# S5's input products on x times the norm's weights; the root and the shift's product applied to their results

## The chip, the cores and the metric

The kernel runs on one core of a Trainium2 chip. The metric is the time of one execution on the device in microseconds. Three runs of the kernel before gave 2488.64, 2485.32 and 2486.29 us, a median of 2486.29.

A core has five engines, each with a queue of its own that runs in the order in which it was written: PE (TensorE, matrix products into PSUM), DVE (VectorE), ACT (ScalarE), POOL (GpSimdE) and SP (SyncE, which here only issues DMA transfers). They wait for one another by semaphores.

## The reference, cut to what matters

x has 512 tokens of 1024 channels. A first network (pool mixer, feed-forward, attention, feed-forward) is followed by a second one, whose first layer is an S5 mixer on a modulated norm of x. Only the lines around the border of the two matter here:

```python
x = x + rms_norm(f, ffn_post_g[layer])            # end of the first network, f from ffn1
...
mod = cond @ ada_w[i] + ada_b[i]                  # cond = silu(c), six parts of 1024 each
sh1, sc1, g1, sh2, sc2, g2 = jnp.split(mod[:, None, :], N_MOD, axis=-1)
h = _modulate(_rmsnorm(x, norm_mix_g[i]), sh1, sc1)   # x * root * g * (1 + sc1) + sh1
...
u = (h @ w_in).astype(f32)                        # S5's input product, w_in is 1024 x 1024
```

With root the reciprocal root of a token's mean square, h @ w_in equals root * ((x * g * (1 + sc1)) @ w_in) + sh1 @ w_in. The root is one number a token, sh1 @ w_in one number a channel.

## The kernel before

x is held transposed: eight tiles xT of 128 channels by 512 tokens. A product in float32 accuracy is made of three matrix products (mm3, L217 to L220): weights and data are each split into a rounded part and the rest (wh and wl; hi and lo), and wh by hi, wh by lo and wl by hi are added in PSUM. Weights come in chunks of 128 x 1024 (wchunk, L178): SP loads ws, ACT makes wh (L203), DVE wl (L204). There are three ws buffers and four each of wh and wl. S5's w_in is split with its columns permuted (perm, L198 to L200), so its reads go in steps of 16 elements.

Between two layers stands a seam (L785). It works by halves of 256 tokens, called half 0 and half 1 here. The layer before finishes its products (for ffn1: tl.run, evacuated by DVE at L979 and squared by ACT at L294, DVE adding up at L295). Then post_add (L426) takes the root of the feed-forward's result, scales it (u, L434) and adds it to xT (L437). A root is made by Norm.rs (L297): PE sums the squares over the channels (L303), ACT takes the root (L305), DVE inverts it and spreads it on a diagonal (L306, L309), and PE spreads it over the partitions (L312); the PSUM tile for it, pn, exists once.

For S5, the seam's second part is a PreNorm (L362): after post_add it needs the squares of the new x, a second root, and then for each of eight tiles u = x * gs * root (DVE, L388), h = u + shift (ACT, L391) and the rest of h (DVE, L392). Only then can the first products of S5 (head, L1406) begin. Elsewhere, before ffn0, attention and ffn1, the seam has a PreScale (L404): it splits x times the norm's weights (L418, L419) in step with post_add, tile by tile, and the root is made later and kept in rsx (L424), to be applied to the products.

S5's head makes four of the eight output tiles of w_in for half 0, then for half 1; the body (L1431) makes the other four for all 512 tokens. u_out (L1331) copies each from PSUM to usc (L1336), writes it to DRAM (d_u) and reads it back in another layout (U), from which states (L1352, products L1360) starts.

The vector mod is made during ffn1 by a background generator: ada_units (L503) calls vecmat (L466), which multiplies rows of ada_w by numbers of cond on DVE. For each of 12 column blocks it takes 8 loads of 256 KB into two buffers (as, L483) and 8 steps (L486, L488) into one accumulator aa; then three rounded copies ab (L496) with two subtractions (L498); then 12 small matrix products into pn (L472) that add over the partitions, and DVE's sum (L475). The blocks not made during ffn1's body are drained before the seam. The order of each engine's queue is fixed when the program is built, by a scheduler that simulates it.

Of the kernel before, what the change touches and what calls it, by code (L numbers as in the profile page):

```python
# [11 lines left out]
F32 = mybir.dt.float32  # L12
# [3 lines left out]
AF = mybir.ActivationFunctionType  # L16
ALU = mybir.AluOpType
# [4 lines left out]
P = 128  # L22
# [3 lines left out]
KD = D // P  # L26
# [36 lines left out]
def net_kernel(ctx: ExitStack, tc: tile.TileContext, I: dict, out: bass.AP, parts=ALL):  # L63
    nc = tc.nc
    V, A, G, T = nc.vector, nc.scalar, nc.gpsimd, nc.tensor

    cst = ctx.enter_context(tc.tile_pool(name="cst", bufs=1))
# [10 lines left out]
    def nm(s):  # L78
        uid[0] += 1
        return f"{s}_{uid[0]}"  # L80
# [4 lines left out]
    def tt(s="t", dt=F32):  # L85
        return tp.tile([P, S], dt, tag="t", name=nm(s))

    def ht(s="h", dt=F32R):
        return hp.tile([P, S], dt, tag="h", name=nm(s))
# [11 lines left out]
    V.memset(ones, 1.0)  # L101
    one16 = cst.tile([P, 1], BF16, name="one16")
    V.memset(one16, 1.0)
    eps1 = cst.tile([P, 1], F32, name="eps1")
    V.memset(eps1, 1e-6)
    eps2 = cst.tile([P, 1], F32, name="eps2")
    V.memset(eps2, 1e-5)
    mod = cst.tile([P, 96], F32, name="mod")
    cond = cst.tile([P, KD], F32, name="cond")
    cond_set = []  # L110
    recent = {}

    nrow = sum(n for _, n in VECS)
    vec = cst.tile([P, nrow], F32, name="vec")
    voff = {}
# [36 lines left out]
    def vc(name, i):  # L152
        o = voff[name] + i
        return vec[:, o:o + 1]

    def md(i, m, k):
        c = i * 48 + m * 8 + k
        return mod[:, c:c + 1]
# [81 lines left out]
    class Held:  # L240
# [3 lines left out]
        def __init__(self, runs):  # L244
            self.runs, self.ch, self.ap = runs, {}, {}
# [109 lines left out]
    def behind(instructions):  # L355

        with ExitStack() as stack:
            for ins in instructions:
                stack.enter_context(tc.issue_after(ins))
            yield  # L360

    class PreNorm:  # L362

        late = False

        def __init__(self, norm, eps, modulate):
            self.norm, self.eps, self.modulate = norm, eps, modulate
            self.h = None
            i, m, gname = modulate
            self.gs = cst.tile([P, KD], F32, tag="gs", bufs=2, name=nm("gs"))  # L370
            c = i * 48 + (m + 1) * 8
            go = voff[gname] + 8 * i
            V.scalar_tensor_tensor(self.gs, mod[:, c:c + 8], 1.0, vec[:, go:go + 8], ALU.add, ALU.mult)

        def parts(self, span):
            return ()
# [27 lines left out]
    class PreScale(PreNorm):  # L404

        late = True

        def __init__(self, norm, eps, gain=None):
            self.norm, self.eps, self.gain = norm, eps, gain
            self.h = [(ht(), ht()) for _ in range(KD)]  # L410
            self.rs = None

        def parts(self, span):

            ts = slice(*span)
            g = [1.0 if self.gain is None else vc(self.gain[0], self.gain[1] + k) for k in range(KD)]
            hi, lo = ([h[i][:, ts] for h in self.h] for i in range(2))
            return (lambda k: A.activation(hi[k], xT[k][:, ts], AF.Copy, scale=g[k]),  # L418
                    lambda k: V.scalar_tensor_tensor(lo[k], xT[k][:, ts], g[k], f(hi[k]), ALU.mult, ALU.subtract))  # L419
# [43 lines left out]

    def vecmat(pool, W, ncb, col, done):  # L466

        def total(parts, cb):
            ps = psn.tile([P, 512], F32, tag="n", name=nm("pn"))
            for j in range(3):  # L470
                for q in range(4):
                    T.matmul(ps[:, 4 * q + j:4 * q + j + 1], parts[j][:, q * P:(q + 1) * P], one16,  # L472
                             start=True, stop=True)
            sums = cst.tile([P, 4], F32, tag="asum", bufs=2, name=nm("sums"))
            V.tensor_reduce(sums, ps[:, :16].rearrange("p (q j) -> p q j", q=4)[:, :, :3], AX.X, ALU.add)  # L475
            done(cb, sums)

        due = None
        for cb in range(ncb):
            acc = None  # L480
            for k in range(KD):
                st = pool.tile([P, 512], F32, tag="as", bufs=2, name=nm("as"))
                nc.sync.dma_start(st, W[k * P:(k + 1) * P, cb * 512:(cb + 1) * 512])  # L483
                if k == 0:
                    acc = pool.tile([P, 512], F32, tag="aa", bufs=1, name=nm("aa"))
                    V.tensor_scalar(acc, st, col(k), None, ALU.mult)  # L486
                else:
                    V.scalar_tensor_tensor(acc, st, col(k), acc, ALU.mult, ALU.add)  # L488
                if k % 2:
                    yield  # L490
                if k == 1 and due is not None:
                    total(*due)
            t2 = tt("ab").bitcast(BF16)
            parts = [t2[:, :512], t2[:, 512:], pool.tile([P, 512], BF16, tag="ab", bufs=1, name=nm("ab"))]
            for j in range(3):
                A.activation(parts[j], acc, AF.Copy)  # L496
                if j < 2:
                    V.tensor_tensor(acc, acc, parts[j], ALU.subtract)  # L498
            due = parts, cb
        yield  # L500
        total(*due)

    def ada_units(pool, i):  # L503

        if not cond_set:
            cond_set.append(True)
            c0 = voff["c_2"]
            with behind([recent["split"]]):
                A.activation(cond, vec[:, c0:c0 + KD], AF.Silu)
            yield  # L510

        def done(cb, sums):
            c = i * 48 + cb * 4
            bo = voff["ada_b_2"] + c
            V.tensor_tensor(mod[:, c:c + 4], sums, vec[:, bo:bo + 4], ALU.add)

        yield from vecmat(pool, I["ada_w_2"][i], 12, lambda k: cond[:, k:k + 1], done)

    def s5_tables(pool, dr):

# [789 lines left out]
    def s5_layer(dr, pool, pa):  # L1310
        S_ = {"gh": [None] * KD, "gl": [None] * KD}
# [19 lines left out]
        def u_out(n, ps, span=FULL):  # L1331
            if span[0] == 0:
                U[n] = tt("usc")
            usc = U[n]
            cs = slice(span[0] // 8, span[1] // 8)
            a = A.activation(usc.rearrange("p (s c) -> p s c", s=8)[:, :, cs], ps.rearrange("p (c s) -> p s c", s=8),  # L1336
                             AF.Copy)
            S_["lastu"] = [a.ins]
            if span[1] < S:
                return  # L1340
            nc.scalar.dma_start(dr["u"][n].rearrange("s (h g c) -> (h g) s c", h=16, g=8),
                                usc.rearrange("p (s c) -> p s c", s=8))
            U[n] = at("U")
            nc.sync.dma_start(U[n], dr["u"][n].rearrange("s (h j) -> (s h) j", h=16))
# [130 lines left out]
        def tail_(hf, nxt):  # L1475
# [23 lines left out]
            for q in range(2):  # L1499
                glu(6 + q, pp[0][:, 256 * q:256 * q + 256], pp[1][:, 256 * q:256 * q + 256], HALVES[hf])  # L1500

        return Layer(lambda nxt: PreNorm(nxt, eps2, (0, 0, "norm_mix_g_2")), load, head, body_, tail_,
                     lambda span, nxt, pre: None)


# [394 lines left out]
    names = [p for p in parts if p != "final"]  # L1900
# [29 lines left out]
        bgps[0] = psmm  # L1930

    rope_c = {}
    s5_on = "s5" in names
    ada_on = [any(p in names for p in q) for q in (("s5", "mlp0"), ("ssd", "mlp1"))]
    ada_due = [i for i in range(2) if ada_on[i]]
    tables_due, toeplitz_due = s5_on, s5_on
# [70 lines left out]
    nxt = None if names[-1] in ("mlp0", "mlp1", "s5", "ssd") else Norm()  # L2007
# [32 lines left out]
```

## Time and profile before

| | |
|---|---|
| median of three runs | 2486.29 us |
| the profiled execution's own time | 2485.38 us |
| its span, first to last instruction | 2483.7 us |
| what lies around the span | 1.7 us |
| PE busy | 2340.7 us, 94% of the span |
| DVE busy | 1713.8 us, 69% |
| ACT busy | 1142.1 us, 46% |
| mean granted TensorE clock | 0.972 |

PE is the engine that sets the time: it is busy nearly throughout, and the places where it stands still are few. One is the seam between ffn1 and S5, from about 1102 to 1185 us of the span. In rows of stretches, each engine's busy time is followed by its instructions in brackets, and PEclk is the granted clock as a share of 2.4 GHz. In rows of the chain the two numbers are the start and the length of a piece in us. Where a row has square brackets, they hold the idle time ahead of the instruction and what ended it.

### The profile page before, as it was taken

The numbers are of one execution on the slowest core, as the hardware profiler recorded it, in microseconds if no ns is written. First come the engines' busy times: TensorE is split into PE (matmuls) and PEld (weight loads), VectorE is DVE, ScalarE is ACT, GpSimd is POOL, SyncE is SP. The second block draws the span as 40 slices with busy tenths as digits, with TensorE's granted clock in tenths as the row PEclk, the third lists the DMA queues.
The fourth block names the chain that finished last, engine by engine and source line by source line (L and its number), as shares of the span: only waits on it lengthen the run. The fifth ranks groups of instructions, "written<-read, shape, count | busy, mean of one in ns | idle before, by whom it ended". The sixth has DMA issues, their size and how long they took to land.

```text
span 2483.7 us, 33557 instructions
## 1 busy us (share of the span) xinstructions
PE 2340.7 (94%) x12397; PEld 1972.1 (79%) x12397; DVE 1713.8 (69%) x3069; ACT 1142.1 (46%) x2038; POOL 337.9 (14%) x345
## 2 busy tenths in 40 slices
PE   7999999788979999986899999999999999999998
PEld 7877777776778888875878887889878888888888
DVE  6896989678658778786655666666777788633333
ACT  6543535467665444344543433334555554422332
POOL 1001223201200000000110210110143331200110
PEclk9999999889989999997999999999999999999999
DMA  4224443311274555552942455543433332232222
GB/s 122 88 88 140 131 142 103 125 52 51 75 206 134 180 178 165 179 173 68 306 153 77 143 166 191 188 134 92 125 105 99 107 104 80 93 102 94 95 88 72
DMA packets 297780, 311.29 MB, mean 125 GB/s; under 512 B 53569, under 2 KB 251025, under 8 KB 296593
## 3 DMA queue, kind: packets, MB, share of 16 engines
q1 hardware_dynamic: 270033, 278.22, 36.0%
q10 hardware_dynamic: 23680, 17.31, 2.3%
q0 software_dynamic: 3904, 13.63, 1.7%
q8 instruction: 97, 1.59, 0.3%
q14 instruction: 66, 0.54, 0.1%
HBM read 284.92 MB, written 24.18 MB: 124 GB/s over the span
## 4 chain that ended last, share of the span: by engine, by line
PE 74%; DVE 12%; DMA 6%; ACT 4%; issue 3%; SPq 0%; POOL 0%; DVEq 0%; ACTq 0%; POOLq 0%
PE mm L219 22%; PE mm L218 22%; PE mm L220 22%; DMA as<-in_ada_w 3%; DVE wl L204 3%; ACT wh L203 1%; DVE aa L488 1%; PE mm L1642 1%; PE mm L1643 1%; PE mm L1644 1%; PE pb L1712 1%; PE pb L754 1%; DMA tz<-d_k 1%; ACT th L775 1%; DMA d_u<-usc 1%
## 5 line engine op out<-in xcount | busy, mean ns | idle before, releaser
L218 PE MATMUL mm<-h,wh 128*128 128x512 f32 (+1 forms) x1792 | 665.6, 374 | 22.9 <-ACT h L418 7.2
L219 PE MATMUL mm<-h,wh 128*128 128x512 f32 (+1 forms) x1792 | 666.1, 372 | 6.2 <-DVE h L392 3.3
L220 PE MATMUL mm<-h,wl 128*128 128x512 f32 (+1 forms) x1792 | 664.8, 372 | 1.7 <-DVE wl L204 1.7
L203 ACT ACTIVATE wh<-ws 128x1024 fp32r<-128x1024 f32 (+1 forms) x367 | 388.0, 1060 | 563.3 <-PE mm L219 479.6
L204 DVE TENSOR_TENSOR wl<-ws,wh 128x1024 fp32r<-128x1024 f32 (+1 forms) x367 | 466.0, 1272 | 240.7 <-ACT wh L203 234.3
L218 PEld LDWEIGHTS mm<-h,wh 128*128 128x128 f32 x1792 | 346.8, 194 | 81.0 <-issue 8.5
L219 PEld LDWEIGHTS mm<-h,wh 128*128 128x128 f32 x1792 | 347.1, 194 | 63.3 <-DVE h L392 5.4
L220 PEld LDWEIGHTS mm<-h,wl 128*128 128x128 f32 x1792 | 347.3, 194 | 56.3 <-DVE wl L204 2.5
L218 PE MATMUL mm<-hi,wh 128*128 128x512 f32 (+1 forms) x1056 | 369.5, 354 | 9.0 <-ACT wh L203 7.6
L219 PE MATMUL mm<-lo,wh 128*128 128x512 f32 (+1 forms) x1056 | 372.0, 353 | 1.7 <-DVE lo L319 1.7
L220 PE MATMUL mm<-hi,wl 128*128 128x512 f32 (+1 forms) x1056 | 370.8, 353 | 0.8 <-DVE wl L204 0.8
L218 PEld LDWEIGHTS mm<-hi,wh 128*128 128x128 f32 x1056 | 200.6, 190 | 37.3 <-ACT wh L203 8.7
L219 PEld LDWEIGHTS mm<-lo,wh 128*128 128x128 f32 x1056 | 201.4, 191 | 28.5 <-DVE lo L319 2.7
L220 PEld LDWEIGHTS mm<-hi,wl 128*128 128x128 f32 x1056 | 201.2, 191 | 26.8 <-DVE wl L204 1.0
L488 DVE SCALAR_TENSOR_TENSOR aa<-as,cond,aa 128x512 f32<-128x512 f32 x168 | 132.0, 786 | 113.8 <-DMA as<-in_ada_w 112.3
L1266 POOL TENSOR_TENSOR r<-r 128x512 f32<-128x512 f32 x64 | 88.1, 1379 | 671.1 <-ACT r L1262 488.0
L760 POOL TENSOR_TENSOR dd<-ident,s5dg 16x64 f32<-16x64 f32 x16 | 69.4, 4337 | 343.1 <-DVE kt L762 336.1
L319 DVE TENSOR_TENSOR lo<-r,hi 128x512 fp32r<-128x512 f32 x64 | 48.1, 756 | 76.5 <-ACT hi L317 76.4
L1287 DVE SCALAR_TENSOR_TENSOR x<-mm,mod,x 128x512 f32<-128x512 f32 (+1 forms) x76 | 48.9, 662 | 60.6 <-PE mm L220 60.4
L496 ACT ACTIVATE ab<-aa 128x512 bf16<-128x512 f32 x72 | 44.9, 624 | 97.0 <-DVE aa L488 61.7
L317 ACT ACTIVATE hi<-r 128x512 fp32r<-128x512 f32 x64 | 40.4, 631 | 72.3 <-POOL r L1266 72.3
L295 DVE TENSOR_TENSOR acc<-acc,sq 128x256 f32<-128x256 f32 (+1 forms) x148 | 62.0, 432 | 16.4 <-ACT sq L294 11.6
(484 smaller groups left out, 3651.2 us busy)
## 6 DMA issues: line engine op xcount, KB each, us to landing
ws<-in_mlp_w SPq DMA_DIRECT2D x124, 512.0 KB, 4.0
as<-in_ada_w SPq DMA_DIRECT2D x192, 256.0 KB, 3.1
ws<-in_ffn_w_in SPq DMA_DIRECT2D x88, 512.0 KB, 3.8
ws<-in_m_w_in SPq DMA_DIRECT2D x41, 512.0 KB, 3.7
ws<-in_ffn_w_out SPq DMA_DIRECT2D x40, 512.0 KB, 3.5
ws<-in_w_o SPq DMA_DIRECT2D x16, 512.0 KB, 3.4
ct<-d_tab SPq DMA_DIRECT2D x8, 1024.0 KB, 9.5
ws<-in_s_w_glu SPq DMA_DIRECT2D x16, 512.0 KB, 5.8
```

What stands on the lines that cost most here:

```text
L203: A.activation(h_, s_, AF.Copy)
L204: V.tensor_tensor(l_, s_, f(h_), ALU.subtract)
L218: T.matmul(ps, wh, xh, start=first, stop=False)
L219: T.matmul(ps, wh, xl, start=False, stop=False)
L220: return T.matmul(ps, wl, xh, start=False, stop=last).ins
L295: V.tensor_tensor(dst, dst, sq[:, a:b], ALU.add)
L319: return hi_, V.tensor_tensor(lo[:, ts], src, f(hi[:, ts]), ALU.subtract)
L488: V.scalar_tensor_tensor(acc, st, col(k), acc, ALU.mult, ALU.add)
L496: A.activation(parts[j], acc, AF.Copy)
L760: G.tensor_tensor(dd, ident[:16, :16].unsqueeze(1).broadcast_to([16, 4, 16]), dg[:, g4].unsqueeze(2).broadcast_to([16, 4, 16]), ALU.mult)
L1266: G.tensor_tensor(r, r, r, ALU.mult)
L1287: V.scalar_tensor_tensor(xT[n][:, ts], ps, md(i, 5, n), xT[n][:, ts], ALU.mult, ALU.add)
```

## The change

S5 takes a PreScale in place of its PreNorm: hi and lo are now parts of x times gs, with gs = g * (1 + sc1), made in step with post_add. The root of x is made later and stored in rsx. A further call of vecmat, behind the twelve blocks of the first mod, multiplies w_in by the shift (two column blocks, 16 loads of 256 KB), with its three copies and two subtractions in the permuted order of the columns; the result is s5c. u_out now multiplies a product by rsx on DVE (new L1356) and adds s5c on ACT (new L1357). The eps constants move into one tile.

```diff
+    def modulated(i, m, gname):
+        gs = cst.tile([P, KD], F32, tag="gs", bufs=2, name=nm("gs"))
+        c = i * 48 + (m + 1) * 8
+        go = voff[gname] + 8 * i
+        V.scalar_tensor_tensor(gs, mod[:, c:c + 8], 1.0, vec[:, go:go + 8], ALU.add, ALU.mult)
+        return gs
...
-        def __init__(self, norm, eps, gain=None):
-            self.norm, self.eps, self.gain = norm, eps, gain
+        def __init__(self, norm, eps, gain=None, modulate=None):
+            self.norm, self.eps = norm, eps
+            if modulate is not None:
+                gs = modulated(*modulate)
+                self.gain = lambda k: gs[:, k:k + 1]
+            else:
+                self.gain = lambda k: 1.0 if gain is None else vc(gain[0], gain[1] + k)
...
+            pv, av = parts, acc
+            if perm:
+                pv = [p_.rearrange("p (a h g) -> p a h g", h=16, g=8) for p_ in parts]
+                av = acc.rearrange("p (a g h) -> p a h g", g=8, h=16)
             for j in range(3):
-                A.activation(parts[j], acc, AF.Copy)
+                A.activation(pv[j], av, AF.Copy)
                 if j < 2:
-                    V.tensor_tensor(acc, acc, parts[j], ALU.subtract)
+                    V.tensor_tensor(av, av, pv[j], ALU.subtract)
...
         yield from vecmat(pool, I["ada_w_2"][i], 12, lambda k: cond[:, k:k + 1], done)
+        if i == 0 and s5_on:
+            yield from vecmat(pool, I["s5_w_in_2"][0], 2, lambda k: md(0, 0, k),
+                              lambda cb, sums: V.tensor_copy(s5c[:, 4 * cb:4 * cb + 4], sums), perm=True)
...
-            a = A.activation(usc.rearrange("p (s c) -> p s c", s=8)[:, :, cs], ps.rearrange("p (c s) -> p s c", s=8),
-                             AF.Copy)
+            t = tt("us")[:, :span[1] - span[0]]
+            V.tensor_tensor(t, ps, S_["pre"].rs[:, slice(*span)], ALU.mult)
+            a = A.activation(usc.rearrange("p (s c) -> p s c", s=8)[:, :, cs], t.rearrange("p (c s) -> p s c", s=8),
+                             AF.Identity, bias=s5c[:, n:n + 1])
...
-        return Layer(lambda nxt: PreNorm(nxt, eps2, (0, 0, "norm_mix_g_2")), load, head, body_, tail_,
+        return Layer(lambda nxt: PreScale(nxt, eps2, modulate=(0, 0, "norm_mix_g_2")), load, head, body_, tail_,
```

Up to the last loads of ada_w in the seam, every queue stands as before. From there on the order differs at three places of weight. PE, end of ffn1's last products, before (mm<-hi,wh are ffn1's products, pn the sums and spreads of a root, mm<-h,wh the first products of S5):

```order
L219 MATMUL mm_10606<-lo_10067,wh_10029 128x256
L220 MATMUL mm_10606<-hi_10066,wl_10030 128x256
L312 MATMUL pn_10356<-dg_10362,ones 128x128 x2
L303 MATMUL pn_10430<-ones,acc_10391 128x128 x2
L312 MATMUL pn_10430<-dg_10436,ones 128x128 x2
L218 MATMUL mm_10793<-h_10414,wh_10752 128x256
```

The root of half 0 is there spread right behind ffn1's last product; its sums (L303) stand 35 products earlier, among them. The same place of the change (line numbers are up by 2 here, and L484 is vecmat's product, before L472):

```order
L484 LDWEIGHTS ab_10215
L484 MATMUL pn_10221<-one_86,ab_10215 128x1
L305 MATMUL pn_10468<-ones,acc_10309 128x128 x2
L314 MATMUL pn_10468<-dg_10474,ones 128x128 x2
L220 MATMUL mm_10860<-h_10247,wh_10819 128x256
L220 MATMUL mm_10917<-h_10247,wh_10831 128x256
L221 MATMUL mm_10860<-h_10248,wh_10819 128x256
L222 MATMUL mm_10860<-h_10247,wl_10820 128x256
```

The sums for half 0's root, now L305, have moved behind all of ffn1's products and behind the 24 small products of the two blocks of s5c; the second root (of x) has gone from between them and S5's products.

ACT at the same place in the change (ab_10167 is the last copy of vecmat's first block of s5c, ab_10214 and ab_10215 the three of its second; acc and sq are the squares of ffn1's half 0, the second acc the first square of half 1; L307 is the root):

```order
L512 ACTIVATE ab_10167<-aa_10143 128x512
L512 ACTIVATE ab_10214<-aa_10175 128x512
L293 ACTIVATE acc_10309<-f_8045 128x256
L296 ACTIVATE sq_10312<-f_8056 128x256
...
L296 ACTIVATE sq_10461<-f_8330 128x256
L296 ACTIVATE sq_10465<-f_8346 128x256
L293 ACTIVATE acc_10309<-f_8045 128x256
L512 ACTIVATE ab_10214<-aa_10175 128x512
L512 ACTIVATE ab_10215<-aa_10175 128x512
```

In the order before, these squares stood behind the first copy of the last block of ada_w; now they stand behind the first copy of the last block of s5c, and so of all that is added up for it.

PE between S5's head and its body, in the change (mm<-... 128x256 is the last of the head for half 1, 128x512 the first of the body):

```order
L220 MATMUL mm_11035<-h_10261,wh_10837 128x256
L221 MATMUL mm_11035<-h_10262,wh_10837 128x256
L222 MATMUL mm_11035<-h_10261,wl_10838 128x256
L314 MATMUL pn_10806<-dg_10812,ones 128x128 x2
L220 MATMUL mm_11112<-h_10247,wh_11115 128x512
L221 MATMUL mm_11112<-h_10248,wh_11115 128x512
```

Before, the body's first product followed the head's last one directly. Now the spread of half 1's root of x, L314, stands between them. DVE in the change, where that root is inverted and put on its diagonal (wl are splits of w_in for the body):

```order
L206 TENSOR_TENSOR wl_11116<-ws_11114,wh_11115 128x1024
L206 TENSOR_TENSOR wl_11146<-ws_11144,wh_11145 128x1024
L206 TENSOR_TENSOR wl_11231<-ws_11229,wh_11230 128x1024
L308 RECIPROCAL sr_10809<-sr_10809 128x2
L311 TENSOR_SCALAR dg_10812<-ident,sr_10809 128x128 x2
L1356 TENSOR_TENSOR us_10910<-mm_10860,rsx_10793 128x256
L206 TENSOR_TENSOR wl_11261<-ws_11259,wh_11260 128x1024
```

Before, the splits of w_in for the body stood there alone; now the inversion and the diagonal stand behind three of them.

## Rows read from the trace of the kernel before

**Rows 1.** Stretches: length, busy PE, PEld, DVE, ACT, POOL, PEclk, DMA share, GB/s.
```profile
1102.00:1114.80 12.80, 12.62 (x109) 12.13 (x107) 10.18 (x18) 8.14 (x8) 2.15 (x5) 1.00 0.69 234
1114.80:1131.10 16.30, 2.39 (x8) 1.85 (x8) 12.48 (x31) 4.81 (x12) 0.50 (x1) 0.60 0.57 201
1131.10:1145.60 14.50, 14.47 (x104) 14.16 (x104) 8.71 (x24) 5.52 (x15) 0.00 (x0) 0.87 0.00 0
1145.60:1159.50 13.90, 2.41 (x10) 1.86 (x9) 10.43 (x29) 4.08 (x11) 0.00 (x0) 0.61 0.00 1
1159.50:1173.90 14.40, 14.40 (x96) 14.26 (x97) 7.90 (x16) 8.57 (x15) 2.50 (x7) 0.78 0.10 36
1173.90:1184.80 10.90, 10.90 (x50) 9.02 (x49) 6.62 (x4) 6.12 (x7) 0.00 (x0) 1.00 1.01 281
1199.00:1232.00 33.00, 26.44 (x214) 25.63 (x212) 22.02 (x30) 17.09 (x27) 7.56 (x15) 0.95 0.88 298
```
**Rows 2.** The chain that ended last, 1060 to 1270 us: start, length, what.
```profile
1093.39 2.69 DMA as<-in_ada_w
1096.17 0.75 DVE aa L488
...
1097.62 0.76 DVE aa L488
...
1103.95 2.01 DVE wl L204
...
1115.52 1.88 DVE wl L204
1117.39 0.78 DVE u L434 x2
...
1126.67 1.21 PE pn L303 x4
...
1130.06 0.49 DVE u L388
...
1131.13 0.79 PE mm L218 x2
...
1145.66 0.87 DVE u L434 x2
...
1199.09 13.74 DMA d_u<-usc
```
**Rows 3.** ACT, instructions in time: a permuted and a plain split of weights.
```profile
1113.52 1.96 ACT L203 ACTIVATE wh<-ws 128x1024 fp32r<-128x1024 f32 x1 [3.02 <-PE mm L219]
...
1186.26 1.06 ACT L203 ACTIVATE wh<-ws 128x1024 fp32r<-128x1024 f32 x1 [2.75 <-PE pv L1360]
```
**Rows 4.** Groups by form: count, busy us, mean ns, idle before.
```profile
L496 ACT ACTIVATE ab<-aa 128x512 bf16<-128x512 f32 x72 | 44.9, 624 | 97.0 <-DVE aa L488 61.7 <-DVE aa L498 35.3
L498 DVE TENSOR_TENSOR aa<-aa,ab 128x512 f32<-128x512 f32 x48 | 36.8, 766 | 15.2 <-ACT ab L496 14.8
L294 ACT ACTIVATE sq<-f 128x256 f32<-128x256 f32 x56 | 19.1, 407 | 0.2
```
**Rows 5.** The chain in the seam from attention to ffn1, a PreScale.
```profile
738.34 0.87 DVE u L434 x2
...
741.45 0.58 PE mm L219
...
755.36 1.23 DVE wl L204
...
757.90 0.50 PE mm L218
```
**Rows 6.** Stretches of PE after its stop at 1145.6: length, busy, PEclk, DMA.
```profile
1146.00:1155.00 9.00, 0.00 (x0) 0.65 0.00 0
...
1162.00:1165.00 3.00, 3.00 (x16) 0.50 0.00 0
1165.00:1168.00 3.00, 3.00 (x24) 0.88 0.34 113
```

More of the change, by code (lines that the diff above doesn't have):

```diff
@@ L103, in net_kernel @@
     V.memset(one16, 1.0)
-    eps1 = cst.tile([P, 1], F32, name="eps1")
+    eps = cst.tile([P, 2], F32, name="eps")
+    eps1, eps2 = eps[:, 0:1], eps[:, 1:2]
     V.memset(eps1, 1e-6)
-    eps2 = cst.tile([P, 1], F32, name="eps2")
     V.memset(eps2, 1e-5)
@@ L109, in net_kernel @@
     cond = cst.tile([P, KD], F32, name="cond")
+    s5c = cst.tile([P, KD], F32, name="s5c")
+    s5_on = "s5" in parts
     cond_set = []
@@ L368, in __init__ @@
             self.h = None
[L369 to L373, printed above, removed]
+            self.gs = modulated(*modulate)
         def parts(self, span):
@@ L415, in parts @@
             ts = slice(*span)
-            g = [1.0 if self.gain is None else vc(self.gain[0], self.gain[1] + k) for k in range(KD)]
+            g = [self.gain(k) for k in range(KD)]
             hi, lo = ([h[i][:, ts] for h in self.h] for i in range(2))
@@ L462, in exp_exact, with vecmat @@
         V.scalar_tensor_tensor(x, q, 1.0, b.bitcast(F32), ALU.add, ALU.mult)
-    def vecmat(pool, W, ncb, col, done):
+    def vecmat(pool, W, ncb, col, done, perm=False):
         def total(parts, cb):
@@ L1932, in net_kernel @@
     rope_c = {}
-    s5_on = "s5" in names
     ada_on = [any(p in names for p in q) for q in (("s5", "mlp0"), ("ssd", "mlp1"))]
```

## The prediction

> **What bounds the kernel now.** I read the table of busy times first. PE works in 94% of the span, so a change pays or costs where PE stands still. Then I cut the border between ffn1 and S5 into stretches [rows 1]. PE is filled to 1114.8 by ffn1's last products, stops for 16.3 us with 2.39 busy, works through the head for half 0 (14.5 us), stops for 13.9 us with 2.41 busy, works through the head for half 1 (14.4), and goes into the body without a stop. These two stops are all that the change can shorten here. The chain of waits names what lies in them [rows 2]: u of post_add at 1117.39 (half 0) and at 1145.66 (half 1), after each the eight tiles of x, the sums of x (1126.67), the first tile of the modulated norm (1130.06), and S5's first product (1131.13). From the first u to the body (1173.9) it is 56.5 us.
>
> The same chain, further up, shows the pace of vecmat: two loads of 256 KB, then two products on DVE, then the next two loads into the same two buffers. From the start of a load (1093.39) to the end of its product (1096.17 + 0.75) it is 3.53 us [rows 2], and the next load into that buffer cannot start earlier: with a little for its issue, I count 3.55 us a pair when nothing else is in its way.
>
> **What the change removes.** Between u of post_add and the first product there is no root and no modulated norm any more. A seam of this form is in the trace already, from attention to ffn1 [rows 5]: from u to the first product it is 3.1 us (738.34 to 741.45), where S5 now needs 13.7 (1117.39 to 1131.13). Half 1's root is no longer made beside the head of half 0: the head's stretch counts 104 products against 96 in that of half 1 [rows 1], and eight of them at about 0.1 us, 0.8 us, leave it (13.7 remain). They come back behind the head as a wait. From sums to a scaled u it is 3.4 us in the chain with four sums and eight squares to add (1126.67 to 1130.06); the two sums of half 1 are half of that, and I take 2.5. From u of half 1 to the body the other seam shows 19.6 us (738.34 to 757.90), head and the wait for half 1's root included.
>
> That last wait is new for S5: the spread of half 1's root stands between head and body, and the DVE work for it stands behind three splits of w_in. Those are permuted here. A permuted split takes 1.96 us on ACT and 1.88 to 2.01 on DVE, a plain one 1.06 and 1.23 [rows 2, 3, 5]. One round of ACT and DVE is ahead of the root in the other seam's chain; with its excess of 0.9 and 0.7, and 1.0 for the splits queued ahead of it, I add 2.6. Bounds are 0, if the splits are done while the head still runs, and 4.8, if all three are in the way. The other seam's own wait there included, PE then stops about 3.6 us ahead of the body.
>
> Sum from u of half 0 to the body: 3.1 + 13.7 + 2.5 + 19.6 + 2.6 = 41.5 us, 15.0 less than 56.5.
>
> **What it adds ahead of that.** The order shows the price. All that post_add of half 0 waits for, the squares of ffn1's result on ACT and the sums on PE, now stands behind the vector product for s5c: behind the first copy of its second block on ACT, behind all 24 small products on PE. ffn1's products end by 1114.8 at the latest [rows 1], and from there PE has nothing else. So I follow the vector product in time.
>
> - The last product of ada_w ends at 1098.4 (1097.62 + 0.76). The two first loads of s5c can follow as buffers come free, but DVE has the first split of w_in ahead of their products: first products at about 1104.6.
> - First block, four pairs. Here SP has between the pairs loads of ws that wait for the splits, and DVE has four splits of 1.9 us between the products. A pair costs 1.9 + 1.5 for the products + 0.7 for adding f and squares + about 1 of waiting at the head of SP's queue, about 5 us; without any of that 3.55. Three pairs behind the first end at about 1120.4.
> - Three copies and two subtractions follow one another. The plain ones take 0.624 and about 0.7 us [rows 4]. Permuted like the splits they become 0.624 x 1.96/1.06 = 1.15 and 0.7 x 1.88/1.23 = 1.1, together about 5.3. The end of the first block's copies is at 1125.7.
> - Second block: its first pair is loaded in the meantime, three more at 3.55 end at about 1137.9 (nothing else stands between them in SP or DVE).
> - Behind its first copy come the squares of half 0, about five of 0.407 ahead of the rest [rows 4], then two copies, two subtractions, 12 products and their sum: 5.3 + 1.9 + 0.3. The sums of half 0's root start at 1145.4 or so, and 3.4 us later u at 1148.8.
>
> Against 1117.39 that is 31.4 us later. Bounds: all pairs at 3.55 from the end of ada_w give 1098.4 + 8 x 3.55 + 5.3 + 0.3 for copies and sums and 3.4 for the root, with the squares hidden, = 1135.8, some 1136, 18.8 later; all eight at 5 us put u at 1155, 38 later. I take the middle case, since the first four pairs have the four splits among them and the last four have not.
>
> [...]
>
> **Terms of the later part.** The granted clock: behind the 13.9 us stop PE ran at 0.50, which is 1.2 GHz, and at 0.88 as a mean between 1165 and 1168 [rows 6]; over the whole head the mean was 0.78 [rows 1], and 0.22 of 14.4 us is 3.2 us lost. Of the stop itself nine us had a mean of 0.65 [rows 6], so it fell early in it. The new stop ahead of the body is about 3.6 us long, and the trace shows none of that length ahead of long products: its cost is 0 if the clock holds, 3.2 if it falls. I take 2, nearer the second.
>
> [...]
>
> The evacuation of each tile is now a product on DVE and then ACT, before its transfer to DRAM: about one DVE instruction of 256 columns later (some 0.4 us, as a u) for the last tile; I take 0.5, at most 2, and at least 0. For the tiles before it, these products lie beside PE's work, where DVE is busy 6.62 of 10.9 us in the body and 7.9 of 14.4 in the head [rows 1]; without that cover each costs the same 0.4. Behind that comes the stretch in which S5 itself waits: from 1199 to 1232 PE is busy 26.4 of 33 us at a DMA share of 0.88 [rows 1], and the write of d_u takes 13.74 us [rows 2]. 4 MB of w_in for s5c and the tables (ct) that stand behind them in SP now share the border, where the shares were 0.57 and then 0.00 for the two stops and the head [rows 1]. Loads that ran in that stretch may be done before it, when PE arrives later: up to the 6.6 us that PE stands there could be given back, nothing at the least. I take 1.5 back, near the low end, since d_u's write keeps its length.
>
> **Sum.** 31.4 - 15.0 + 2 + 0.5 - 1.5 = 17.4, about +17 us. The profiled execution took 2485.38 us (2483.7 of span and 1.7 around it), so it becomes 2502.4; the median of the runs is 0.9 above it, so 2503. The bounds of the vector product alone make it +5 and +24; those of the four smaller terms (0 to 4.8, 0 to 3.2, 0 to 2, and 0 to 6.6 off) can move it by another 4 or 5 either way. The case's own range is thus +1 to +29, 2487 to 2515.
>
> **The rivals.**
> 1. *The vector product is hidden (other side).* If the loads run while ffn1's products still fill PE, u of half 0 stays near 1117.4, the 15.0 us are kept, and with +2 and +0.5 the sum is -13, 2473. For it: two buffers are free from 1098, and the transfers stood at 0.69 and 0.57 of their capacity until 1131 [rows 1]. Against it: 16 loads, in pairs of 3.55, need 28.4 us and only 16.4 are left to 1114.8. For the full gain a pair would have to take 0.8 us; the sum changes its sign at 2.5 us a pair, or at 3.0 with plain copies.
> 2. *Only the loads count.* DVE and SP never hold a pair up: 18.8 - 15.0 + 2 + 0.5 - 1.5 = about +5, 2491. For it: DVE was busy only 12.48 of 16.3 us in the first stop [rows 1]. Against it: in the order the splits stand between its products.
> 3. *The loads are slower.* Loads of ws, rot and ct at the same time stretch a pair to 5 us throughout, the clock falls and nothing is given back: 38 - 15.0 + 3.2 + 2 = about +28, 2514. For it: 281 GB/s was full load in the body's stretch, a share of 1.01 [rows 1]. Against it: while S5's chunks were loaded and split, in the first stop, it was 201.
> 4. *S5 gives it back.* The 6.6 us of standing in 1199 to 1232 vanish, since its loads are there early: 17.4 + 1.5 - 6.6 = about +12, 2499. For it: the DMA share of 0.88 there. Against it: d_u can only start when the head is done, and takes 13.74 us by itself.
>
> **Chances.** The forecast 0.50; hidden 0.06; only loads 0.18; slower loads 0.12; given back 0.14. A change under 0.2% (5 us) is about what a measurement of this kernel cannot tell from none. Faster by more: the first rival, 0.06. Within it: half of the second, 0.09, and a little of the others, 0.10 in all. Slower by more: 0.84. The range reaches from the second rival's low side to the third: 2487 to 2516.
>
> **What would show it.** Right: PE stands from about 1115 to 1145, its first wait ended by copies of ab or by products of aa; the pairs of s5c's first block take about 5 us and those of its second about 3.6; a permuted copy takes about 1.1 us; the wait between the heads falls from 13.9 to about 6; a new stop of some 3.6 us lies ahead of the body, with a granted clock of 0.5 behind it; the first product of states comes about 18 us after 1184.85 (the body's stretch ends at 1184.8). Wrong: u of half 0 before 1125, which would mean that the transfers of s5c ran beside ffn1 or in pairs far under 3.5 us; a wait between the heads over 10 us; no stop before the body; or a gain of over 6 us in S5's own stretches after 1199.

## The result, and the profile after

The changed kernel took 2513.01 us, the median of four runs (2509.92 to 2513.89); the kernel before, run beside it, 2485.81 us (2482.91 to 2488.64). The ratio is 1.0107, with a 95% interval of 1.009 to 1.0125: 27 us slower, inside the stated range (2487 to 2516), and 10 us above the predicted 2503. The profiled execution has a span of 2510.1 us against 2483.7.

The stretches of the seam in the profile after, with the columns of [rows 1]:

```profile
1114.50:1154.69 40.19, 4.10 (x33) 2.96 (x32) 21.03 (x36) 10.55 (x17) 1.08 (x3) 0.53 0.46 153
1154.69:1171.20 16.51, 14.13 (x97) 13.64 (x98) 13.94 (x38) 8.35 (x23) 0.00 (x0) 0.79 0.19 77
1171.20:1187.70 16.50, 13.18 (x84) 12.53 (x84) 12.98 (x37) 8.13 (x19) 0.00 (x0) 0.79 0.00 0
1191.70:1198.10 6.40, 0.82 (x7) 0.53 (x5) 5.73 (x9) 3.69 (x6) 0.00 (x0) 0.81 0.74 244
1198.10:1202.40 4.30, 4.30 (x10) 3.43 (x11) 1.92 (x6) 3.85 (x6) 1.84 (x5) 0.50 0.51 159
```

The first stop of PE is now 40.19 us long with 4.10 busy, where it was 16.3 with 2.39. The 13.9 us between the heads have shrunk: half 1's first product starts at 1175.24, 3.94 us after half 0's last one has ended (about 6 had been said), and from 1171.2 to 1187.7 PE is busy 13.18 of 16.5 us. A new stop of 6.4 us with 0.82 busy stands ahead of the body, and behind it PE runs at a granted clock of 0.50 for 4.3 us. The chain of waits of the profile after shows what lies in the first stop (start, length, what):

```profile
1104.98 0.48 DVE aa L498
...
1106.27 6.98 DMA as<-in_s_w_in
...
1117.25 6.42 DMA as<-in_s_w_in
...
1124.54 0.76 DVE aa L500
1125.33 1.07 ACT ab L512
1126.42 1.03 DVE aa L514
...
1131.21 2.60 DMA as<-in_s_w_in
...
1135.82 3.08 DMA as<-in_s_w_in
...
1142.73 0.76 DVE aa L500
1143.52 1.07 ACT ab L512
...
1151.27 1.24 PE pn L305 x4
...
1154.69 0.87 DVE u L445 x2
...
1173.44 0.87 DVE u L445 x2
...
1195.81 1.89 DVE wl L206
1197.70 0.34 DVE us L1356
...
```

These answer to [rows 2]. Nearly all of it is the vector product for s5c: its first block's loads (6.98 and 6.42 us for 256 KB, where a load of ada_w took 2.69), its copies, its second block's loads, its last copies. Only then come the sums for half 0's root (L305) and u (1154.69, before 1117.39). The last rows belong to the stop ahead of the body. PE's instructions there, the idle time ahead of each and what ended it in square brackets:

```profile
1194.80 0.68 PE L314 MATMUL pn<-dg,ones 128*128 128x128 f32 x4 [2.97 <-DVE dg L311]
1198.09 0.79 PE L220 MATMUL mm<-h,wh 128*128 128x512 f32 x1 [2.61 <-DVE us L1356]
```

PE waits first for half 1's root, then for a PSUM tile that DVE empties (us) behind the split of 1195.81.

Term by term, from the two profiles:

| term | predicted | measured | from |
|---|---|---|---|
| u of half 0 | 31.4 later | 37.3 later | 1117.39 to 1154.69 |
| from it to u of half 1 | 19.3 us | 18.75 (28.3 before) | 1154.69, 1173.44 |
| on to the body's first product | 22.2 us | 24.65 (28.3 before) | 1198.09 |
| on to the first product of states | 13.4 us | 13.1 (10.9 before) | 1211.18 |
| the rest | 1.5 shorter | 0.0 | what is left of the spans' difference |
| sum | +17.4 | +26.4 | 2510.1 - 2483.7 |

### The profile page after: what moved, and what is told of

It reads as the page before. It is cut to its first block, busy times and chain, and to the rows that moved or that the text cites. A ratio compares the mean times of both kernels' runs of the same rounds, so it can differ in the third digit from the quotient of the medians.

```text
span 2510.1 us, 33668 instructions
## 1 busy us (share of the span) xinstructions
PE 2345.1 (93%) x12421; PEld 1975.3 (79%) x12421; DVE 1725.1 (69%) x3089; ACT 1154.0 (46%) x2046; POOL 340.8 (14%) x345
## 4 chain that ended last, share of the span: by engine, by line
PE 65%; DVE 12%; issue 9%; DMA 7%; ACT 4%; POOL 1%; SPq 0%; ACTq 0%; DVEq 0%; POOLq 0%
PE mm L221 19%; PE mm L220 19%; PE mm L222 19%; DMA as<-in_ada_w 3%; DVE wl L206 2%; DVE aa L500 1%; ACT wh L205 1%; DMA as<-in_s_w_in 1%; DMA tz<-d_k 1%; PE mm L1663 1%; PE mm L1664 1%; PE mm L1665 1%; PE pb L1733 1%; PE pb L773 1%; POOL r L1285 1%
## 5 line engine op out<-in xcount | busy, mean ns | idle before, releaser
L220 PE MATMUL mm<-h,wh 128*128 128x512 f32 (+1 forms) x1792 | 665.9, 374 | 27.0 <-ACT h L429 10.9
L205 ACT ACTIVATE wh<-ws 128x1024 fp32r<-128x1024 f32 (+1 forms) x367 | 388.0, 1060 | 555.2 <-PE mm L221 473.4
L221 PEld LDWEIGHTS mm<-lo,wh 128*128 128x128 f32 x1056 | 202.8, 192 | 26.6 <-DVE lo L321 0.8
L512 ACT ACTIVATE ab<-aa 128x512 bf16<-128x512 f32 x78 | 51.3, 658 | 123.9 <-DVE aa L500 85.9
```

The source lines that it names most:

```text
L205: A.activation(h_, s_, AF.Copy)
L220: T.matmul(ps, wh, xh, start=first, stop=False)
L221: T.matmul(ps, wh, xl, start=False, stop=False)
L512: A.activation(pv[j], av, AF.Copy)
```

## The experiments

Each run stands beside runs of the kernel before on the same chip. The medians of before were 2491.9 to 2496.3 us in these three sets of runs, so ratios and their 95% intervals are compared (a difference in us is the ratio's, times the median of before in its set), and positions in a trace by their distance from an event in the same trace.

**no_shift: the change without its vector product.**

```diff
+    V.memset(s5c, 0.0)
-        if i == 0 and s5_on:
+        if False:
```

> The change with its vector product left out: s5c is set to zero, so the shift's product with w_in is not computed. Theory (the 27 us are the vector product in the seam, which puts u of half 0 off by 37.3 us, less what the PreScale gives back between that u and the body, 56.5 - 43.4 = 13.1 us, with some 2 us of it lost again to the clock behind the stop ahead of the body): u of half 0 near 1117 as before, the body's first product near 1161, and a time of about 2476 us, 10 below the kernel before. Rival (the PreScale's own stop ahead of the body and the longer evacuation eat what it gains, and the vector product costs less than 37): within 3 us of the kernel before or slower.

Measured: 0.9957 (0.9937 to 0.9977), 10.7 us less than before, with an interval of 5.7 to 15.7. DVE's first u of each half:

```profile
1121.53 0.87 DVE L446 SCALAR_TENSOR_TENSOR u<-f,vec,pn 128x256 f32<-128x256 f32 x2
...
1140.30 0.87 DVE L446 SCALAR_TENSOR_TENSOR u<-f,vec,pn 128x256 f32<-128x256 f32 x2 [0.67 <-PE pn L315]
```

The halves are 18.77 us apart as in the change (18.75), and not 28.3 as before. Both positions came late: u of half 0 4 us behind the theory's 1117, the body's first product at 1164.09 instead of 1161. But from the one to the other it is 42.6 us, where it was 56.5 before. The PreScale by itself gains what the theory said; the rival, that its own stop eats this, falls.

**before_vec: the kernel before with the vector product alone**, called behind the twelve blocks as in the change, S5's norm left as it was.

> The kernel before with the vector product for s5c added at the same place, its result unused, and S5's norm left as it was. Theory: u of half 0 is put off by about 37 us, nothing is gained behind it, so about 2523 us (+37), up to 5 less where S5's transfers come early. Rival (the vector product is worth about 27 and the PreScale nothing): 2513 us or less.

Measured: 1.0147 (1.0126 to 1.0169), 36.7 us more (31 to 42); the theory said 37. The two parts add within these intervals: 36.7 - 10.7 = 26.0, and the change cost 26.6.

**rate5 and before_rate5: faster stepping.** The generator is called with 5 instead of 3 steps at each column pair of ffn1, in the change and in the kernel before.

```diff
-            layer = ffn_layer(1, ((0, 8), (8, 16), (16, 22)))
+            layer = ffn_layer(1, ((0, 8), (8, 16), (16, 22)), rate=5)
```

> The change as it is, with the background generator stepped five times instead of three at each of ffn1's column pairs, so that both blocks of s5c are done before ffn1's last products end. Theory (the vector product costs time only because PE has nothing to do beside it): as the kernel without the vector product, about 2476 us, at most 8 us more if ffn1's own waits grow. Rival (its 4 MB of loads and its work on DVE and ACT cost the same wherever they lie, since transfers are what is short): 2500 us or more.

> The kernel before with the faster stepping alone, the control for the run above. Theory: the last blocks of ada_w leave the seam's start, but u of half 0 is set by ffn1's products and the first root there, so 0 to 3 us are gained, 2483 to 2486 us. Rival (the stepping is itself worth a lot, or costs ffn1 time): a change of more than 5 us either way.

Measured: 1.0051 (1.0031 to 1.0072) for both. Both theories failed: neither did the change come out at 2476, nor was the control within 3 us of before (it was 13 above, as its rival had it). What PE waited for in ffn1 in rate5 (us in total, times, longest):

```profile
PE pn L484 <- ACT ab L512: 16.0, 5, 7.7
PE mm L220 <- ACT wh L205: 3.5, 1, 3.5
```

The small products that add up a block wait in PE's queue for ACT's copies, with ffn1's products behind them. In the kernel before this wait was 1.4 us in all; with five steps it is 16.0 us in the change and 17.6 in the control. The rival (transfers are short wherever the loads lie) had the time nearly right, but the control, which has none of these 4 MB, shows the same time and the same wait.

**late_rate4: four steps, and the small products issued later.**

```diff
-                if k == 1 and due is not None:
+                if k == 7 and due is not None:
...
-            layer = ffn_layer(1, ((0, 8), (8, 16), (16, 22)))
+            layer = ffn_layer(1, ((0, 8), (8, 16), (16, 22)), rate=4)
```

> The change with two edits: the generator is stepped four times instead of three in ffn1, and the small products on PE that add up a block are issued six loads later (at the last row pair of the next block instead of the first), long after their copies. In the kernel with five steps PE stood 16.0 us in front of five such products, waiting for ACT's copies, with ffn1's products queued behind them. Theory (that queue order was the whole price of the faster stepping): the waits of PE for ab fall under 3 us, u of half 0 comes within 4 us of its place in the kernel before, and with the PreScale's gain the time is 5 to 10 us below before. Rival (DVE, ACT or the transfers are what ffn1 lacks when vecmat runs faster): still 5 us or more above before.

Measured: 0.9984 (0.9974 to 0.9994), 4 us less than before (1.5 to 6.5), just short of the 5 to 10 that the theory had. PE's waits in ffn1:

```profile
PE mm L220 <- DVE u L958: 8.8, 3, 3.4
PE mm L220 <- ACT wh L205: 2.4, 2, 1.4
...
PE pn L484 <- ACT ab L512: 0.8, 1, 0.8
```

The wait for ab is gone (0.8 us), as the theory said. The run has four steps and rate5 five, so it does not tell how much of this is the later issue and how much the slower stepping. 8.8 us for DVE's u (L958) have come in its place; before_late4 below has 7.2 us of the same wait without the product for s5c, so it goes with the stepping. From u in the seam ahead of ffn1 to u of half 0 it is 387 us (738.59 to 1125.65), 8 more than before (379), where the theory had allowed 4: the vector product was hidden for the most part, not wholly.

**plain: the copies for s5c in plain order**, so that the channels of s5c stand in another order than those of the products (pv = parts, av = acc).

> The change with vecmat's copies and subtractions for s5c in plain order; the channels of s5c are then in the wrong order, so the output differs in the shift's part. Theory: the three copies and two subtractions of a block take 3.3 us instead of 5.3 measured, both blocks stand on the path to u of half 0, which comes 4 us earlier; about 23 us above before instead of 27. Rival (the loads of the next block fill that time anyway, so only the second block's copies count): 25.

Measured: 1.0108 (1.0091 to 1.0125), as the change. The chain of waits shows the shorter copies:

```profile
1130.29 0.64 ACT ab L512
1130.95 0.70 DVE aa L514
```

0.64 and 0.70 instead of 1.07 and 1.03. From the last product of ada_w (1103.87 + 0.74) to u of half 0 (1156.47) it is 51.9 us, against 55.6 in the change (1099.1 to 1154.69): 3.7 less, near the theory's 4; the first block's loads and products took nearly as long (19.8 us, 20.3 in the change). The time does not show it: the interval is about 4 us to either side, as wide as the effect. In the time the run is inconclusive.

**tabs_late and vt_late: the loads of S5's tables later.** In tabs_late the first two calls of tabs and the first of ctabs move from the head's load to the body; the scheduler still sent vt's loads, on POOL's queue, at the old place. In vt_late all of them are on SP, behind the last load of as.

```diff
-                    nc.gpsimd.dma_start(vt[n][i], dr["tab"][n][:, 1024 + 512 * i:1536 + 512 * i])
+                    nc.sync.dma_start(vt[n][i], dr["tab"][n][:, 1024 + 512 * i:1536 + 512 * i])
...
+            with behind([recent["as"]]):
```

> The change with the loads of S5's tables 0 and 1 (rot, vt, ct; about 3 MB) moved from ahead of the head to the start of the body. Theory (the loads of as took 6.98 and 6.42 us in the first block since tables and chunks of w_in moved at the same time): they fall to under 5 us, u of half 0 comes 3 to 5 us earlier, and the time is 22 to 25 us above before, if S5's first outputs do not wait for ct. Rival (as is late because SP, in its order, waits for splits ahead of it): loads as long as before, u of half 0 as before, and S5 loses by the late tables, 28 us or more.

> The change with every load of S5's tables (vt, rot, ct), vt's included, put behind the last load of as in SP's queue; the run with late tables had left vt's loads, on POOL's queue, where they were. Theory (in the first block of s5c the transfers are what is short: chunks of w_in, tables and as at once, at a DMA share near 0.9): loads of as in that block fall to 4.5 us or less, the stretch from the last product of ada_w to u of half 0, 55.6 us in the change, becomes about 50, and the time is 20 to 24 us above before. Rival (the chunks of w_in alone fill the transfers, or SP's waits hold as up): 54 us or more, and 26 us above before.

Measured: tabs_late 1.0133 (1.0117 to 1.0148), 33 us above before, with loads as long as in the change, as its rival had said; vt_late 1.0099 (1.0085 to 1.0113), 24.7, between its theory (20 to 24) and its rival (26). In vt_late the transfers had more room. One stretch, with the columns of [rows 1], first of the change, then of vt_late:

```profile
1104.00:1126.00 22.00, 10.59 (x91) 10.35 (x89) 14.39 (x20) 6.70 (x4) 2.66 (x5) 0.80 0.78 257
```

```profile
1104.00:1126.00 22.00, 13.09 (x116) 12.71 (x114) 16.84 (x22) 9.13 (x7) 0.00 (x0) 0.90 0.58 191
```

A DMA share of 0.58 instead of 0.78, and the eight products of the first block took 16.4 us (1106.63 to 1123.0) instead of 20.3 (1104.98 to 1125.3). From the last product of ada_w to u of half 0 it is 51.8 us, and 55.6 in the change: most of the way to the 50 of the theory. The run fix (below) took 16.3 us (1108.26 to 1124.58) although its loads of rot stand where the change has them. But its POOL queue differs: the scheduler, which orders all queues anew for every kernel, put fewer loads of vt (256 KB each) there. POOL's rows at the first block, of the change:

```profile
1101.36 0.54 POOL L1340 DMA_DIRECT2D vt<-d_tab  x1 [98.01 <-PE mm L222]
1106.14 0.54 POOL L1340 DMA_DIRECT2D vt<-d_tab  x1 [4.24 <-PE mm L222]
1113.46 2.12 POOL L1340 DMA_DIRECT2D vt<-d_tab  x4 [6.78 <-PE mm L221]
```

In fix the first two stand there too (1104.27, 1109.05), the four others not. All runs that make the vector product in the seam, sorted by the number of vt loads issued between the last product of ada_w and the end of the first block:

| run | loads of vt | first block, us | last product of ada_w to u of half 0, us |
|---|---|---|---|
| vt_late | 0 | 16.4 | 51.8 |
| fix | 2 | 16.3 | 51.9 |
| raw | 4 | 17.8 | 53.3 |
| plain (shorter copies) | 6 | 19.8 | 51.9 |
| before_vec | 6 | 20.0 | 55.1 |
| the change | 6 | 20.3 | 55.6 |
| tabs_late (no rot) | 8 | 20.9 | 56.3 |

From the seam ahead of ffn1 to the end of that block the change, fix, raw, plain and before_vec have the same instructions in the same order on PE, DVE, ACT and SP. So the block's length goes with the loads of vt, and not with those of rot: about 4 us for six of them. Each line is one execution, and no run moved vt's loads by intent alone. Taking them out of the block did not shorten the kernel, since S5 pays later: from the first product of states to the last py it is 82.5 us in tabs_late, 83.6 in vt_late and 79.3 in fix, 77.0 in the change.

**raw: the head's tiles copied out of PSUM by ACT first.**

```diff
+            if span != FULL:
+                A.activation(t, ps, AF.Copy)
+                ps = t
             V.tensor_tensor(t, ps, S_["pre"].rs[:, slice(*span)], ALU.mult)
```

> The change with the head's tiles copied from PSUM by ACT as soon as they are made, the product with the root done in place on the copy afterwards. Theory (the body's first product, at 1198.09, stood 2.61 us for a PSUM tile which DVE empties only behind the root of half 1 and the fourth split of w_in): that wait goes, the stop ahead of the body falls from 6.4 to about 3.8 us, and the time is about 24 us above before. Rival (without it PE waits for the body's split weights instead): 27 as the change.

Measured: 1.0135 (1.012 to 1.015), 34 us above before. PE at the body:

```profile
1199.25 0.79 PE L220 MATMUL mm<-h,wh 128*128 128x512 f32 x1 [3.70 <-ACT us L1357]
```

The wait changed its engine and grew from 2.61 to 3.70 us: the copy stands in ACT's queue behind the splits there. Theory and rival both fall. S5's own part also grew, to 82.8 us; here too POOL's order changed, with two loads of vt less in the first block.

**fix: the splits for the body queued behind the evacuation.**

```diff
+                if j < KD - 2:
...
+                    late[0]()
+                    with behind([S_["us0"]]):
+                        late[1]()
+                else:
+                    with behind([S_["us1"], S_["pre"].root]):
+                        for split_ in late:
+                            split_()
```

> The change with the splits of w_in for the body's second half queued behind the evacuation of the head (on DVE behind the last product with the root, on ACT behind rsx), and the second split of the body's first half behind the evacuation of half 0. Theory (PE's stop of 6.4 us ahead of the body, 1191.67 to 1198.09, is DVE's queue order: root of half 1 and evacuation behind four splits): the stop falls to about 2 us, the clock does not fall behind it, the first product of states comes 5 to 6 us earlier against u of half 1, about 21 us above before in all. Rival (the body then waits for its own splits, or the clock falls all the same): stop over 4 us, 25 us or more above before.

Measured: 1.0108 (1.0095 to 1.0122), no better than the change. The stop ahead of the body is gone: the body begins at 1191.88, right behind the root's spread. The stretch of its first ten us, and in PE's instructions the first product of states:

```profile
1191.80:1202.00 10.20, 10.12 (x45) 8.38 (x46) 7.70 (x10) 9.39 (x11) 4.17 (x6) 1.00 0.54 165
```

```profile
1210.65 1.62 PE L1381 MATMUL pv<-U,vt 128*128 128x128 f32 x6 [7.60 <-DMA U<-d_u]
```

PE is full and its clock stays at 1.00, as the theory said, and then it stands 7.60 us for U. From u of half 1 to the first product of states it is 37.2 us (1173.48 to 1210.65), in the change 37.7 (1173.44 to 1211.18). In fix the path there is not PE's but the evacuation's: the root of half 1, us, usc, the write of d_u, the read of U. ACT issued the first d_u at 1200.83 in the change and at 1199.17 in fix. Two things besides the root hold that path up in fix. ACT makes two splits of weights (3.90 us from 1192.48) between rsx of half 1 and the usc that need it. And the loads of vt that fix did not make in the first block are issued beside d_u's writes. POOL's queue, the chain's row of the last of these writes, and the stretch:

```profile
1199.86 1.06 POOL L1340 DMA_DIRECT2D vt<-d_tab  x2
1200.96 1.06 POOL L1340 DMA_DIRECT2D vt<-d_tab  x2
1202.06 1.06 POOL L1340 DMA_DIRECT2D vt<-d_tab  x2
```

```profile
1201.22 12.53 DMA d_u<-usc
```

```profile
1199.00:1211.00 12.00, 4.40 (x20) 3.38 (x19) 3.69 (x5) 6.31 (x8) 4.13 (x9) 0.85 1.05 332
```

The DMA share is 1.05 there; in the change, which issues two loads of vt at that place, it is 0.90 from 1200.8 to 1211.2. The read of U behind the last write is issued at 1213.76, in the change at 1209.31. For the first product of states the second write and the read behind it count: 5.89 and 4.84 us in fix, 5.29 and at most 4.35 in the change, so this part of the way was at least 1.1 us longer. The theory failed (the product was to come 5 to 6 us earlier); the rival's time held, but neither of its reasons, a stop or a clock that falls. What fix would gain with the loads of vt where the change has them, no run shows. ACT's issue in the kernel before:

```profile
1173.66 1.01 ACTq L1341 DMA_DIRECT2D d_u<-usc  x2
...
```

There the first write was issued 0.3 us ahead of the body's first product (1173.93); in the change it stands 2.7 us behind it, since the evacuation waits for half 1's root.

**fix_late4 and before_late4: the best of both, and its control.** fix_late4 joins fix and late_rate4; before_late4 is the kernel before with late_rate4's two edits.

> Both edits that should help, in one: the generator stepped four times in ffn1 with the small products issued six loads later, and the splits behind the evacuation as in the run fix. Theory (the two costs lie in different stretches and add): 4 us below before from the first, measured, and some 5 us more from the second, about 9 us below before. Rival (S5's transfers wait for the same point whatever comes earlier): no better than the first alone, 4 us below.

> The kernel before with the faster stepping and the later small products alone, the control for the run above. Theory (in the kernel before both lie hidden, its u of half 0 follows from ffn1's products): within 3 us of before. Rival (the later small products are worth most of the gain by themselves): 4 us or more below before.

Measured: fix_late4 0.9981 (0.9972 to 0.999), no more than late_rate4 alone (0.9984), as its rival said. PE waits 7.91 us for U there, with six loads of vt beside d_u's writes as in fix. before_late4 0.9951 (0.9938 to 0.9963), 12 us below before: the control's theory failed, and its rival was right. Which of its two edits gives this, no run separates. The two edits help the changed kernel more (from 1.0107 to 0.9984, about 31 us) than the kernel before, yet the fastest kernel of all is without the change. On the same chip fix_late4 had a median of 2489.5 us and before_late4 2482.3. From u in the seam ahead of ffn1 to u of half 0 it is 384.9 us against 370.9; from there to the first product of states 58.9 against 72.6; from that to the last py 79.1 against 74.6. So 14.0 more, 13.7 less and 4.5 more, and 3.7 more in the rest of the two profiled executions. Of the 14.0 us some is still the vector product's end, which the chain to u of half 0 in fix_late4 runs over:

```profile
1112.89 1.05 ACT ab L512
1113.99 0.25 PE pn L484 x4
1116.86 0.45 PE pn L305 x4
```

## Why the prediction came out as it did

- *Sign and mechanism: shown.* That the price is the vector product ahead of half 0's root, and that the PreScale gains behind it, is what no_shift and before_vec measure separately: -10.7 and +36.7. The time lay inside the range, but 10 us above the forecast, and nearly all of that is three terms that erred the same way: 5.9 us for the vector product, 1.9 for the PreScale, 1.5 for what S5 was to give back.
- *The vector product, 31.4 us: mis-sized, 37.3.* The steps before and behind the first block held: first product at 1104.98 (1104.6 said), copies of a block 5.35 us (5.3), second block 12.8 (12.2), from its last product to u 11.2 (10.9). The failed term is the first block's pace, 5 us a pair: the block ended 20.3 us after its first product, where 15.8 had been said. The price was made of DVE's work and SP's waits, and POOL's queue was not in it; the rows show loads of 6.98 and 6.42 us, beside four loads of vt issued from 1113.46 on. With none or two of these in the block (vt_late, fix) it takes 16.4 and 16.3 us, near the forecast. Rival 3, slower loads, gave 2514 and so came nearest to the time. Its mechanism holds for the first block, with vt's loads in place of the rot and ct that it named; the second block's pairs took 3.7 to 4.6 us, not 5 (3.55 had been forecast). In fix the block had the forecast's pace and the time was no better: u of half 0 came 3.7 us sooner behind ada_w, but S5's part, with vt's loads beside d_u's writes, took 2.3 us more.
- *The PreScale's 15.0 us: 13.1.* From u to u it is 18.75 (19.3 said). One reading in that sum was wrong: 741.45 is the third product of the other seam; its first stands at 740.14, 1.8 us behind u, and in the change it is 1.8 as well (1156.49). The stop ahead of the body came, with 6.4 instead of 3.6 us, and with a reason the forecast did not have: besides the root PE waited there for a PSUM tile, whose emptying had become DVE's work and stood behind a split.
- *The clock: right.* 2 us were said; from 1198.1 on 4.3 us ran at 0.50, which is 2.15 us lost, less than the 3.2 us that a fall was to cost. For the GHz named ahead of the result the runs give an estimate: products of 128x512 in the profile after start 0.426 us apart at 0.50 (1198.68 to 1202.09), 1.2 columns a ns, which read as one column a clock gives 1.2 GHz, and doubled 2.4; at 1.00 they start 0.23 us apart (1203.00 to 1203.92).
- *Evacuation, 0.5 us: its size held by luck, its path was not seen.* From the body's first product to the first product of states the change takes 13.1 us, 10.9 as before and 2.15 for the clock, so nothing is left for this term. But it was costed as one more instruction on PE's path, at the body, and PE's stop of 6.4 us covered a second path. The evacuation waits for half 1's root, and a DRAM round trip hangs on it: in fix, without that stop, PE stands 7.60 us for U and the first product of states comes only 0.5 us earlier. How much of this is the root and how much the splits on ACT and the loads of vt in its way stays open.
- *Given back, 1.5 us: wrong.* S5 took 1.2 us longer (77.0 against 75.8 from the first product of states to the last py); what lies behind it was 1.2 us shorter. Rival 4 falls.
- *Rival 1, the hidden vector product (-13): half right.* Hidden for the most part (late_rate4) the change is 4 us below before. But what is left of it ahead of u of half 0, 14.0 us in fix_late4, is as much as the PreScale gains (13.7): with the same stepping the kernel without the change is 7 us faster.

Open: whether the change would gain from fix with vt's loads in a place where neither the first block nor d_u's writes need the transfers. S5's 4.5 us more in fix_late4 than in its control have no cause shown here.

## What to carry to other kernels

A product moved out of a chain has to be made somewhere: ask first how long its loads are at the pace of the buffers that they go through, and what already fills that place, on every queue; 4 MB through two buffers cost 37 us where the chain it shortened gave back 11. Follow a deferred scale to the first consumer of the scaled values, not to the end of the product: if that consumer is a write and a read of DRAM, a stop of the matrix engine removed there can come back as a wait for the read, as the 7.60 us in fix. Where a scheduler orders the queues anew, compare all of them before an edit is credited or blamed: here loads of vt moved with edits elsewhere. And give the kernel before every edit that helps the new one: here such a control gained 12 us and was the best version.

## What the runs showed that was not expected

- Products that wait in PE's queue for a late copy cost far more than they take: 0.27 us each group, 16.0 us of waiting in ffn1 with five steps, 0.8 us with four steps and an issue six loads later.
- The pace of the first block went with loads on a queue that the forecast did not look at: eight loads and products took 16.3 to 20.9 us with 0 to 8 loads of vt beside them, and one load of 256 KB up to 9.15 us (tabs_late, 8 loads of vt).
- The granted clock was 0.50 behind the change's stop of 6.4 us with 0.82 busy, and 0.50 from 1175.24 to 1182 behind the 3.94 us between the heads with 1.13 busy. In fix PE was busy 11.67 of the 11.8 us ahead of 1191.8, and the clock stayed at 1.00 in the ten us behind.
